# A two-layer trunk with expert mixtures: requests for expert weights, the split of the tokens and the order within a group of experts are changed

## The chip, the core and the metric

The kernel runs on one core of a Trainium2 chip. The metric is the time of one execution on the device in microseconds. TensorE (PE) multiplies matrices into PSUM banks, VectorE (DVE), ScalarE (ACT) and GpSimd (POOL) work element by element, and SyncE (SP) issues nearly all transfers, in the order of its queue; a request whose target is not yet free holds up all behind it. All arithmetic is in float32.

## The reference

There are 256 context tokens and 256 latent tokens of 1024 channels and two layers. Layer 0 mixes with attention beside a gated delta rule, layer 1 with a recurrence over the tokens; after each comes a mixture of experts, over 512 tokens in layer 0 and over the 256 latent tokens in layer 1:

```python
def hier_moe(h, w_group, b_group, w_expert, b_expert, w1, w3, w2):
    pg = softmax(h @ w_group + b_group)          # 4 groups of experts, the best is taken
    pg_top, g_idx = lax.top_k(pg, 1)
    pe = softmax(take_along_axis(h @ w_expert + b_expert, sel, axis=1))   # the group's 8 experts
    pe_top, e_loc = lax.top_k(pe, 2)             # the two best
    wts = pg_top * pe_top / jnp.sum(pe_top, -1, keepdims=True)
    ...                                          # tokens sorted by expert
        hid = jax.nn.silu(xb @ w1[e]) * (xb @ w3[e])
        return out.at[toks].add((hid @ w2[e]) * ws[:, None]), None
```

w1 and w3 of an expert are 1024 x 512, w2 is 512 x 1024: 2 MiB each, 6 MiB an expert, 32 experts a layer.

## The kernel before

A pool of 21 tiles of 1 MiB (128 partitions x 2048 float32, called s in the rows) holds the activations h, the weights and other large data. An expert matrix fills two tiles; `weight` (L163) issues one request for each. Tiles are given out by a planner, which also fixes the order of the instructions on each engine: it takes the code's order as priority and works with its own estimate of the times. `issue_after` and a dependency set by hand bind it.

Between mixer and mixture, `project_out` (L904; for layer 1 the end of `mixer1`, L1646) asks for the output weights, the rows of shift and scale (`rows`, L377), and the first expert weights (`moe_ahead`, L628: six matrices in layer 0, w1, w3 and w2 of experts 0 and 1, and five in layer 1). While the projection runs, `tokens` (L389) makes the logits and the transposed tokens, `raw`. Its inner function `split` (L430) then makes the normalized, shifted tokens for each of the token tiles: a rank-one matmul of a row of ones with the shift, and a matmul of `raw` with a diagonal of the token norms, both into one PSUM bank. ACT copies the bank, rounded, to the upper half `hi` of a tile of f, and DVE subtracts it for the lower half `lo`, so that the gather can use two fast passes.

`moe` (L645) runs the router (L454; its last instruction is `last`), builds the first group's one-hot matrix P, calls `split`, then in layer 0 `sort` (L518), which orders the experts 4 to 31 by their token count (experts 0 to 3 are fixed), and `overflow`. Then come the groups, two in flight: in layer 0 pairs of experts (64 tokens each), one group of 96 and 32, and three groups of four experts (32 tokens each); in layer 1 eight groups of four. A group gathers its tokens (L681), multiplies by w1 and w3 (L705), transposes, multiplies by w2 (L729), splits the result into y and scatters it into h (L739). Within these matmuls each expert writes its own partitions of the bank, that is, it uses its own columns of PE; the four experts (or parts of 32) follow one another inside the loop over k. For w2 the order is half of the output, k, expert; for the last group of a layer it is expert, k, half (L728).

Weights are asked for expert by expert (L704, L723). For the sorted experts SP first loads the expert's number into a register (`value_load`, L772). In layer 1 the first six groups stand ahead of a loop for experts with more tokens than their place, which here runs no time, and the last two behind it; five matrices of the seventh group are asked for ahead of the loop (L798). In layer 0 the loop stands behind all groups; the next mixer's first weights (`mixer1_weights`, L1429) are asked for ahead of it.

Of the kernel before, what the change touches and what calls it, by code (L numbers as in the profile page):

```python
# [118 lines left out]
class Trunk:  # L119
# [43 lines left out]
    def weight(self, src, natural=False, eng=None):  # L163
# [11 lines left out]
        return ks  # L175

# [212 lines left out]
    def tokens(self, l, h, lo, rows):  # L389
# [40 lines left out]
        def split(last):  # L430

            f = []
            dg = self.tmp(nt * 128).rearrange("p (t n) -> p t n", t=nt)
            for t in range(nt):
                self.act(dg[:, t], self.c["ident"], AF.Copy, scale=rs[:, t:t + 1])
                f.append(self.slot().rearrange("p (i n) -> p i n", i=2))
            for i in range(2):
                half = slice(512 * i, 512 * i + 512)
                for t in range(nt):
                    ps = self.bank()  # L440
                    add = rows[st(t)][0:1, 1, 4 * i:4 * i + 4].rearrange("p k n -> p (k n)")
                    self.mm(ps, self.c["ones"][0:1], add, True, False)
                    self.mm(ps, dg[:, t], raw[t][:, half], False, True)
                    hi, lo = f[t][:, 0, half], f[t][:, 1, half]
                    if i:
                        with self.tc.issue_after(last.ins):
                            self.split(hi, lo, ps)
                    else:
                        self.split(hi, lo, ps)
            return f  # L450
# [143 lines left out]
    def job(self, l, nt, sid, w, table, P):  # L594
# [30 lines left out]
        load = lambda name, g: self.weight(I[name][l, bass.ds(ereg, 1)].rearrange("o a b -> (o a) b"))  # L625
        return wt[:, :, None], load

    def moe_ahead(self, l):  # L628

        G = 2 if l == 0 else 4  # L630
        names = [(n, e + g) for e in (0, G) for n in ("moe_w1", "moe_w3", "moe_w2") for g in range(G)]
        return {(n, e): self.weight(self.I[n][l, e]) for n, e in names[:(6, 5)[l]]}

    def split(self, hi, lo, a, eng=None):

        self.act(hi.bitcast(F32R), a)
        self.tt(lo.bitcast(F32R), a, hi, OP.subtract, eng)

# [6 lines left out]
    def moe(self, l, h, lo, ahead, tokens, then=None):  # L645
# [3 lines left out]
        logits, split = tokens  # L649
        sid, w, cnt, last, chosen = self.router(logits, nt)  # L650
# [18 lines left out]
        def group(P, wt, load, caps, last=False):  # L669
# [31 lines left out]
            for i in range(2):  # L701
                ps = self.bank()
                hp.append(ps)
                W = [load(("moe_w1", "moe_w3")[i], g) for g in range(G)]  # L704
# [18 lines left out]
            W = [load("moe_w2", g) for g in range(G)]  # L723
            pw = [self.bank() for _ in range(2)]
            order = [(i, k, q) for i in range(2) for k in range(4) for q in parts]
            if last:

                order = [(i, k, q) for q in parts for k in range(4) for i in range(2)]  # L728
# [18 lines left out]
        def experts(spec, last):  # L747
# [17 lines left out]
            regs = {}  # L765

            def load(name, g):
                p = cols[g]
                if p < fixed:
                    return ahead.pop((name, p), None) or self.weight(I[name][l, p])  # L770
                if p not in regs:
                    regs[p] = nc.sync.value_load(order[0:1, p:p + 1], min_val=0, max_val=31)  # L772
                return self.weight(I[name][l, bass.ds(regs[p], 1)].rearrange("o a b -> (o a) b"))

            yield from group(P, weights[:, :, cs], load, caps, last)

        def extra():
            P = t4()
            wt, load = self.job(l, nt, sid, w, table, P)
            yield  # L780
            yield from group(P, wt, load, (128,))

        gens = [experts(s, i == len(specs) - 1) for i, s in enumerate(specs)]
        next(gens[0])
        ft = split(last)
        next(gens[0])
        rank = None
        if l == 0:
            sp, wp, order, rank = self.sort(nt, sid, cnt, chosen)
# [6 lines left out]
        else:  # L796
            e0 = specs[cut][0][0]
            for name, g in [(m, g) for m in ("moe_w1", "moe_w3") for g in range(4)][:5]:  # L798
                ahead[name, e0 + g] = self.weight(I[name][l, e0 + g])
# [1290 lines left out]
```

## Time and profile before

| | |
|---|---|
| median of 3 runs | 2273.4 us (2269.46 to 2273.95) |
| profiled execution | 2272.61 us, its span 2270.8 us |
| PE busy | 1849.2 us, 81% of the span |
| DVE, ACT, POOL busy | 849.9, 546.5, 363.3 us |
| read from and written to device memory | 537.66 and 34.90 MB, 252 GB/s over the span |
| requests for expert weights | 384 of 1 MiB |
| mean granted clock of TensorE | 0.852 of full speed |

Times in the rows count from the span's start. Busy time says how long an engine had an instruction in work; neighbouring matmuls overlap, so a busy PE need not be at its peak, and the duration of a run of matmuls is better read from its first start to its last end. A float32 matmul appears as two records. The granted clock (PEclk) is 1.00 at 2.4 GHz and 0.50 at 1.2 GHz. The share of the DMA engines can read 1.01.

### The profile page before, as it was taken

How to read it: one execution, taken by the hardware profiler on the slowest of the kernel's cores; microseconds unless marked ns; L12 is line 12 of the kernel's file. 1: busy time of each engine (PE TensorE's matmuls, PEld its weight loads, DVE VectorE, ACT ScalarE, POOL GpSimd, SP SyncE). 2: the span in 40 equal slices, each digit the busy share in tenths (PEclk: the TensorE clock that was granted, in tenths of full speed). 3: DMA queues.
4: the chain of work that ended last, by engine and by line, in shares of the span. 5: the costliest groups of instructions: out<-in, count | busy, mean ns of one | idle time of the engine just before them, and what ended most of it. 6: DMA issues, size and time to landing. Idle time of an engine off the chain costs nothing.

```text
span 2270.8 us, 32125 instructions
## 1 busy us (share of the span) xinstructions
PE 1849.2 (81%) x12738; PEld 1020.6 (45%) x12738; DVE 849.9 (37%) x1889; ACT 546.5 (24%) x1110; POOL 363.3 (16%) x603
## 2 busy tenths in 40 slices
PE   5996888898999898998599698789786877666577
PEld 2443566566444343443245466657675422222222
DVE  3357345533332223221644856565822311111101
ACT  3363223320211111111324524425221100000000
POOL 1034145310000000000403732234400000000000
PEclk7998889899899999999797686578575788788789
DMA  9631132760099999999252544372774399999995
GB/s 308 225 130 38 43 112 100 268 245 22 12 422 421 421 421 421 421 421 392 73 195 79 186 140 154 121 237 77 277 268 178 133 422 421 421 422 421 384 422 248
DMA packets 161226, 574.70 MB, mean 253 GB/s; under 512 B 26218, under 2 KB 61073, under 8 KB 108593
## 3 DMA queue, kind: packets, MB, share of 16 engines
q1 hardware_dynamic: 158704, 572.36, 65.1%
q8 instruction: 102, 1.67, 0.3%
q10 hardware_dynamic: 2369, 0.25, 0.1%
q14 instruction: 51, 0.42, 0.1%
HBM read 537.66 MB, written 34.90 MB: 252 GB/s over the span
## 4 chain that ended last, share of the span: by engine, by line
DMA 19%; PE 18%; DVE 8%; ACT 3%; issue 2%; POOL 1%; SPq 0%; ACTq 0%; DVEq 0%; POOLq 0%
PE b L202 18%; DMA s<-in_moe_w 16%; DVE s L184 3%; ACT t L197 2%; DVE kb L184 1%; DVE t L184 1%; DVE s L193 1%; PE b L213 1%; ACT s L197 1%; DMA s<-vD 1%; POOL s L184 1%; DMA s<-in_rk_wr 1%; POOL t L184 0%; DVE s L1977 0%; DMA s<-kD 0%
## 5 line engine op out<-in xcount | busy, mean ns | idle before, releaser
L202 PE MATMUL b<-s 64*64 64x64 f32 (+10 forms) x5840 | 671.0, 324 | 103.2 <-DVE s L193 27.1
L202 PEld LDWEIGHTS b<-s 128*64 128x64 f32 (+5 forms) x5840 | 444.3, 184 | 331.9 <-issue 173.9
L202 PE MATMUL b<-s,kb 128*32 128x512 f32 (+1 forms) x2112 | 365.4, 649 | 80.3 <-DMA s<-in_moe_w 80.3
L202 PE MATMUL b<-s,t 128*32 128x512 f32 (+4 forms) x1544 | 349.5, 566 | 50.4 <-DMA s<-in_moe_w 24.6
L197 ACT ACTIVATE t<-b 128x512 f32<-128x512 f32 (+3 forms) x161 | 91.3, 571 | 715.5 <-PE b L202 422.1
L202 PEld LDWEIGHTS b<-s,t 128*32 128x32 f32 (+2 forms) x1544 | 153.6, 148 | 212.0 <-issue 129.1
L202 PEld LDWEIGHTS b<-s,kb 128*32 128x32 f32 (+1 forms) x2112 | 97.3, 125 | 324.8 <-issue 207.9
L197 ACT ACTIVATE s<-b 128x256 f32<-128x256 f32 (+6 forms) x194 | 101.0, 526 | 463.4 <-PE b L202 425.7
L202 PE MATMUL b<-t,s 128*128 128x512 f32 (+3 forms) x592 | 160.4, 424 | 19.5 <-ACT s L197 8.9
L184 DVE TENSOR_TENSOR s<-b,s 128x512 fp32r<-128x512 f32 (+2 forms) x86 | 52.3, 626 | 274.5 <-ACT s L197 266.1
L193 DVE SCALAR_TENSOR_TENSOR s<-b,mcol,s 128x256 f32<-128x256 f32 x296 | 120.9, 476 | 80.8 <-PE b L202 80.6
L213 PE MATMUL b<-cst,t 128*128 128x128 f32 (+1 forms) x466 | 80.3, 304 | 75.6 <-DVE t L193 35.1
L202 PEld LDWEIGHTS b<-t,s 128*128 128x128 f32 (+2 forms) x592 | 100.7, 205 | 79.5 <-ACT s L197 26.3
L184 POOL TENSOR_TENSOR t<-t 128x256 f32<-128x256 f32 (+1 forms) x20 | 21.0, 1052 | 651.9 <-DMA hD<-s 534.0
L213 PEld LDWEIGHTS b<-cst,t 128*128 128x128 f32 (+1 forms) x466 | 57.4, 162 | 121.4 <-issue 42.9
L193 DVE SCALAR_TENSOR_TENSOR t<-t,wc,b 128x512 f32<-128x512 f32 x21 | 15.7, 747 | 201.2 <-PE b L202 201.2
L213 PE MATMUL b<-cst,s 128*128 128x128 f32 (+1 forms) x332 | 60.7, 323 | 23.6 <-DVE s L184 14.8
L193 DVE SCALAR_TENSOR_TENSOR t<-t,b 128x512 f32<-128x512 f32 x21 | 14.4, 688 | 169.6 <-ACT t L197 169.6
L197 ACT ACTIVATE kb<-b 128x512 f32<-128x512 f32 (+2 forms) x92 | 49.9, 545 | 100.2 <-PE b L202 66.8
L202 PE MATMUL b<-t,cst 128*128 128x512 f32 (+6 forms) x64 | 37.2, 699 | 44.0 <-POOL t L184 20.0
L213 PEld LDWEIGHTS b<-cst,s 128*128 128x128 f32 (+1 forms) x332 | 46.3, 168 | 39.4 <-issue 28.5
L202 PE MATMUL b<-s,cs 128*32 128x512 f32 x384 | 54.9, 655 | 6.5 <-DMA s<-in_ada_w 6.0
(240 smaller groups left out, 1637.4 us busy)
## 6 DMA issues: line engine op xcount, KB each, us to landing
s<-in_moe_w SPq DMA_DIRECT2D x384, 1024.0 KB, 19.8
s<-in_ada_w SPq DMA_DIRECT2D x48, 1024.0 KB, 8.5
s<-in_hy_w_in SPq DMA_DIRECT2D x8, 1024.0 KB, 5.0
sD<-s SPq DMA_DIRECT2D x8, 1024.0 KB
s<-zD SPq DMA_DIRECT2D x8, 1024.0 KB, 7.6
s<-sD SPq DMA_DIRECT2D x8, 1024.0 KB, 10.1
s<-in_hy_w_out SPq DMA_DIRECT2D x4, 1024.0 KB
s<-in_rk_wk SPq DMA_DIRECT2D x4, 1024.0 KB, 8.7
```

Source lines behind the costliest of these rows:

```text
L184: (eng or self.nc.vector).tensor_tensor(out=out, in0=a, in1=b, op=op)
L193: self.nc.vector.scalar_tensor_tensor(out, a, s, b, op0=op0, op1=op1)
L197: self.nc.scalar.activation(out, a, func, bias=bias, scale=scale)
L202: return self.nc.tensor.matmul(out, lhsT, rhs, start=start, stop=stop, skip_group_check=skip)
L213: self.nc.tensor.transpose(out, a, self.c["ident"][:n, :n])
```

## The change

`weights` loads several matrices side by side: the first tile of each, then the second of each. `moe_ahead` uses it; layer 0 asks for the same six matrices, layer 1 for w1 and w3 of four experts. `split` becomes a generator: the first half of the channels (matmuls and `hi`) is traced ahead of the router, its `lo` and the second half's matmuls behind it. In layer 0 all weights of experts 2 and 3 are asked for ahead of `sort`. A register load is tied behind the request that was traced before it (`late_load`). Ahead of layer 1's loop four matrices are asked for instead of five. The w2 order is k, half, expert for all groups.

```diff
+    def weights(self, srcs):
+        n = srcs[0].shape[1]
+        nk, per = srcs[0].shape[0] // 128, 2048 // n
+        out = [[] for _ in srcs]
+        for k0 in range(0, nk, per):
+            for ks, src in zip(out, srcs):
+                t = self.slot().rearrange("p (k n) -> p k n", n=n)
+                self.nc.sync.dma_start(t, src.rearrange("(p k) n -> p k n", p=128)[:, k0:k0 + per])
+                ks += [t[:, i] for i in range(per)]
+        return out
...
-        def split(last):
-            f = []
+        def split():
+            f = [self.slot().rearrange("p (i n) -> p i n", i=2) for _ in range(nt)]
             dg = self.tmp(nt * 128).rearrange("p (t n) -> p t n", t=nt)
             for t in range(nt):
                 self.act(dg[:, t], self.c["ident"], AF.Copy, scale=rs[:, t:t + 1])
-                f.append(self.slot().rearrange("p (i n) -> p i n", i=2))
             for i in range(2):
                 half = slice(512 * i, 512 * i + 512)
+                pss = [self.bank() for _ in range(nt)]
                 for t in range(nt):
-                    ps = self.bank()
                     add = rows[st(t)][0:1, 1, 4 * i:4 * i + 4].rearrange("p k n -> p (k n)")
-                    self.mm(ps, self.c["ones"][0:1], add, True, False)
-                    self.mm(ps, dg[:, t], raw[t][:, half], False, True)
-                    hi, lo = f[t][:, 0, half], f[t][:, 1, half]
+                    self.mm(pss[t], self.c["ones"][0:1], add, True, False)
+                for t in range(nt):
+                    self.mm(pss[t], dg[:, t], raw[t][:, half], False, True)
+                    self.act(f[t][:, 0, half].bitcast(F32R), pss[t])
+                last = yield
+                for t in range(nt):
                     if i:
                         with self.tc.issue_after(last.ins):
-                            self.split(hi, lo, ps)
+                            self.tt(f[t][:, 1, half].bitcast(F32R), pss[t], f[t][:, 0, half], OP.subtract)
                     else:
-                        self.split(hi, lo, ps)
-            return f
+                        self.tt(f[t][:, 1, half].bitcast(F32R), pss[t], f[t][:, 0, half], OP.subtract)
+            yield f
...
     def moe_ahead(self, l):
         G = 2 if l == 0 else 4
-        names = [(n, e + g) for e in (0, G) for n in ("moe_w1", "moe_w3", "moe_w2") for g in range(G)]
-        return {(n, e): self.weight(self.I[n][l, e]) for n, e in names[:(6, 5)[l]]}
+        names = ("moe_w1", "moe_w3", "moe_w2")[:3 - l]
+        return {(n, g): w for n in names for g, w in enumerate(self.weights([self.I[n][l, g] for g in range(G)]))}
...
+    def late_load(self, ap, top):
+        ins = self.nc.cur_bb.bb.instructions
+        n = len(ins)
+        prev = next(i for i in reversed(ins) if i.engine == mybir.EngineType.SP)
+        v = self.nc.sync.value_load(ap, min_val=0, max_val=top)
+        first = next(i for i in ins[n:] if i.engine == prev.engine)
+        self.tc.add_manual_dep(first, prev.name, ...)
+        return v
...
         logits, split = tokens
+        split = split()
+        next(split)
         sid, w, cnt, last, chosen = self.router(logits, nt)
...
-                W = [load(("moe_w1", "moe_w3")[i], g) for g in range(G)]
+                W = loads(("moe_w1", "moe_w3")[i])
...
-            W = [load("moe_w2", g) for g in range(G)]
+            W = loads("moe_w2")
             pw = [self.bank() for _ in range(2)]
-            order = [(i, k, q) for i in range(2) for k in range(4) for q in parts]
-            if last:
-                order = [(i, k, q) for q in parts for k in range(4) for i in range(2)]
+            order = [(i, k, q) for k in range(4) for i in range(2) for q in parts]
...
+        regs = {}
+        def fetch(name, cols):
+            if (name, cols[0]) in ahead:
+                return [ahead.pop((name, p)) for p in cols]
+            srcs = []
+            for p in cols:
+                if p < fixed:
+                    srcs.append(I[name][l, p])
+                    continue
+                if p not in regs:
+                    regs[p] = self.late_load(order[0:1, p:p + 1], 31)
+                srcs.append(I[name][l, bass.ds(regs[p], 1)].rearrange("o a b -> (o a) b"))
+            return self.weights(srcs)
...
         next(gens[0])
-        ft = split(last)
+        split.send(last)
+        ft = split.send(last)
         next(gens[0])
         rank = None
         if l == 0:
+            for name in ("moe_w1", "moe_w3", "moe_w2"):
+                ahead.update({(name, p): x for p, x in zip((2, 3), fetch(name, (2, 3)))})
             sp, wp, order, rank = self.sort(nt, sid, cnt, chosen)
...
-            e0 = specs[cut][0][0]
-            for name, g in [(m, g) for m in ("moe_w1", "moe_w3") for g in range(4)][:5]:
-                ahead[name, e0 + g] = self.weight(I[name][l, e0 + g])
+            cols = specs[cut][0]
+            for name in ("moe_w1",):
+                ahead.update({(name, p): w for p, w in zip(cols, fetch(name, cols))})
```

## Rows read from the trace of the kernel before

**Rows 1.** The page, 40 slices of the span: what the transfers moved.
```profile
GB/s 308 225 130 38 43 112 100 268 245 22 12 422 421 421 421 421 421 421 392 73 195 79 186 140 154 121 237 77 277 268 178 133 422 421 421 422 421 384 422 248
```
**Rows 2.** Stretches: their length, each engine's busy time (instructions), granted clock, DMA share, GB/s.
```profile
497.00:621.30 124.30, 113.00 (x394) 73.22 (x395) 41.41 (x141) 17.27 (x32) 4.83 (x4) 0.90 0.04 11
...
621.30:1061.30 440.00, 397.28 (x2155) 183.86 (x2153) 122.04 (x282) 61.50 (x105) 0.00 (x0) 1.00 1.01 419
...
1084.00:1088.00 4.00, 3.43 (x15) 2.79 (x16) 2.33 (x6) 0.51 (x1) 0.00 (x0) 1.00 0.08 31
...
2244.00:2248.00 4.00, 4.00 (x14) 1.17 (x14) 0.00 (x0) 0.00 (x0) 0.00 (x0) 1.00 0.27 113
```
**Rows 3.** SP's queue in time order, 461 to 622 us: start, length, line, transfer.
```profile
461.00 89.08 SPq L173 DMA_DIRECT2D s<-in_moe_w  x12
...
561.94 0.29 SPq L1416 DMA_DIRECT2D t<-in_rk_ln_b  x1
621.28 0.85 SPq L173 DMA_DIRECT2D s<-in_moe_w  x2
```
**Rows 4.** The register loads of L772: nanoseconds min/median/max, first and last start in us.
```profile
L772 SPq TENSOR_LOAD <-o_int x28: 262/264/477, 604.8 to 620.6; - x28
L772 SPq FUSED_REGOPS  x28: 147/147/181, 605.3 to 621.0; - x28
```
**Rows 5.** SP's waits from 480 to 700 us: us in total, times, longest.
```profile
SPq L772 <- DVE t L184: 42.9, 1, 42.9
```
**Rows 6.** PE in time order at the start of layer 0's mixture [idle before <- releaser].
```profile
558.10 1.84 PE L202 MATMUL b<-cst,t 128*128 128x1 f32 x16
...
568.87 14.02 PE L202 MATMUL b<-s,cst 1*128 1x512 f32 x16
582.82 10.72 PE L202 MATMUL b<-s,t 128*128 128x512 f32 x24
...
599.37 14.00 PE L202 MATMUL b<-s,kb 128*64 128x512 f32 x64
```
**Rows 7.** Stretches of the same place, columns as in rows 2: the granted clock.
```profile
562.00:563.00 1.00, 0.00 (x0) 0.00 (x0) 0.90 (x8) 0.22 (x1) 0.00 (x0) 0.73 0.05 12
...
568.00:582.00 14.00, 14.00 (x20) 5.81 (x20) 2.82 (x16) 0.00 (x0) 0.00 (x0) 0.50 0.00 1
...
586.00:587.00 1.00, 1.00 (x3) 0.38 (x2) 0.25 (x1) 0.42 (x1) 0.00 (x0) 0.82 0.00 0
```
**Rows 8.** PE in time order, layer 0's groups: a w2, two quads, the last w2.
```profile
694.24 7.07 PE L202 MATMUL b<-s,t 128*32 128x512 f32 x64
...
741.39 7.92 PE L202 MATMUL b<-s,kb 128*32 128x512 f32 x70
752.13 7.05 PE L202 MATMUL b<-s,kb 128*32 128x512 f32 x58 [2.82 <-DMA s<-in_moe_w]
...
891.08 7.92 PE L202 MATMUL b<-s,kb 128*32 128x512 f32 x70
...
1061.29 22.59 PE L202 MATMUL b<-s,t 128*32 128x512 f32 x64 [0.69 <-ACT t L197]
```
**Rows 9.** PE in time order, layer 1: start of the mixture and its last w2.
```profile
1773.92 1.71 PE L213 MATMUL b<-cst,s 128*128 128x128 f32 x8
...
1789.52 7.29 PE L202 MATMUL b<-s,t 128*128 128x512 f32 x12
...
2240.06 19.16 PE L202 MATMUL b<-s,t 128*32 128x512 f32 x56
```
**Rows 10.** SP's queue: the next mixer's first stores, and loads of the recurrence.
```profile
1093.45 4.24 SPq L1448 DMA_DIRECT2D hD<-s  x8
...
1723.75 1.49 SPq L1891 DMA_DIRECT2D s<-vD  x2
```
**Rows 11.** DVE behind layer 1's loop, in time order.
```profile
2149.02 0.76 DVE L184 TENSOR_TENSOR t<-cst,r_sid 128x256 fp32r<-128x256 f32 x2 [15.92 <-DMA s<-in_moe_w]
```
**Rows 12.** PE's waits from 620 to 1100 us: us in total, times, longest.
```profile
PE b L202 <- DMA s<-in_moe_w: 11.0, 6, 3.4
```

More of the change, by code (lines that the diff above doesn't have):

```diff
@@ L624, in job @@
         ereg = nc.sync.value_load(reg_t, min_val=0, max_val=31)
-        load = lambda name, g: self.weight(I[name][l, bass.ds(ereg, 1)].rearrange("o a b -> (o a) b"))
-        return wt[:, :, None], load
+        loads = lambda name: self.weights([I[name][l, bass.ds(ereg, 1)].rearrange("o a b -> (o a) b")])
+        return wt[:, :, None], loads
     def moe_ahead(self, l):
         G = 2 if l == 0 else 4
-        names = [(n, e + g) for e in (0, G) for n in ("moe_w1", "moe_w3", "moe_w2") for g in range(G)]
-        return {(n, e): self.weight(self.I[n][l, e]) for n, e in names[:(6, 5)[l]]}
+        names = ("moe_w1", "moe_w3", "moe_w2")[:3 - l]
+        return {(n, g): w for n in names for g, w in enumerate(self.weights([self.I[n][l, g] for g in range(G)]))}
     def split(self, hi, lo, a, eng=None):
@@ L637, in split @@
         self.tt(lo.bitcast(F32R), a, hi, OP.subtract, eng)
+    def late_load(self, ap, top):
[4 more added lines that the diff above has]
+        first = next(i for i in ins[n:] if i.engine == prev.engine)
+        self.tc.add_manual_dep(first, prev.name, mybir.DependencyInfo(mybir.DependencyClass.NoSync,
+                                                                      mybir.DependencyReason.DATA), reason="late_load")
+        return v
     def pick(self, out, onehot, hi, lo, start=True, stop=True):
@@ L667, in moe, with group @@
         half = lambda i: slice(512 * i, 512 * i + 512)
-        def group(P, wt, load, caps, last=False):
+        def group(P, wt, loads, caps):
             G = len(caps)
@@ L745, in group, with experts @@
                     yield
-        def experts(spec, last):
+        regs = {}
[11 more added lines that the diff above has]
+            return self.weights(srcs)
+        def experts(spec):
             cols, caps = spec
@@ L764, in experts @@
             yield
[L765 to L775, printed above, removed]
+            yield from group(P, weights[:, :, cs], lambda name: fetch(name, cols), caps)
         def extra():
             P = t4()
-            wt, load = self.job(l, nt, sid, w, table, P)
+            wt, loads = self.job(l, nt, sid, w, table, P)
             yield
-            yield from group(P, wt, load, (128,))
-        gens = [experts(s, i == len(specs) - 1) for i, s in enumerate(specs)]
+            yield from group(P, wt, loads, (128,))
+        gens = [experts(s) for s in specs]
         next(gens[0])
-        ft = split(last)
+        split.send(last)
+        ft = split.send(last)
         next(gens[0])
```

## The prediction, made before the changed kernel was run

> **What bounds the kernel now.** I began with the page's forty slices [rows 1]. The DMA engines run at about 421 GB/s in slices 11 to 17 and 32 to 37 and far lower elsewhere. These two stretches are the two expert mixtures. Each must read 32 experts of 6 MiB, 192 tiles of 1 MiB; at 421 GB/s a tile takes 2.49 us, so a mixture costs 478 us of transfer however it is ordered. What can be won is time in which the queue stands still while weights are wanted, and work that is left once the last tile is there.
>
> The second view was SP's queue at the first mixture's start [rows 3]. Twelve tiles (experts 0 and 1) are asked for between 461 and 550 us; the next request goes out at 621.28 us. In the stretch from 497 to 621.3 us DMA is 4% busy, in the 440 us behind it 101% [rows 2]. Two things fill the end of that hole: SP waits 42.9 us for the sorted order [rows 5], then issues 28 register loads [rows 4] back to back from 604.8 to 621.3 us, though the next 12 tiles (experts 2 and 3) need no register. TensorE (PE), meanwhile, finishes the logits at 559.94 us, waits for the router, and only then does the split's matmuls [rows 6].
>
> The third view was PE at the mixtures' ends. In all other groups of four column parts, 64 down-projection records take 7.07 us, 0.110 us each, because neighbours in the order use different column parts. The last group runs part by part: 22.59 us for the same 64 in layer 0 [rows 8], and 19.16 us for the last 56 in layer 1 [rows 9]. There DMA ends at about 2245.1 us (113 GB/s over the 4 us from 2244 [rows 2] is 1.1 us at full rate), and PE at 2259.2 us.
>
> **Which time the sum uses.** The profiled execution took 2272.6 us with a span of 2270.8 us; the median of the runs is 2273.4 us, 0.8 us more. I work on 2272.6.
>
> **Split ahead of the router, layer 0.** Eight rank-one matmuls of the row of ones (16 records) and eight of the raw tokens (16 records) move. Before, the ones begin at 568.87 us and cost 14.02 us, 0.876 us a record; the raw tokens' records end 2.1 us (eight gather records) before 593.54 us, at 591.4 us; expert matmuls start at 599.37 us [rows 6], 8.0 us later. In the new order the ones can start at 559.94 us. The granted clock stays 1.00 for 2.7 us of PE's pause, then falls to 0.50 (1.2 GHz) [rows 7]. It stays there through 14 us in which PE is busy with the ones alone, and comes back to 1.00 (2.4 GHz) about 3.4 us after the raw tokens start at 582.82 us. I take it that the ones don't hold the clock: 2.8 us at 0.43 us a record does 6.4 records, the other 9.6 take 8.4 us (571.1 us); the router's two matmuls 1.2 us (572.3); raw tokens 3.4 us at 0.50 for 3.9 records, then 12.1 at 0.43, 5.2 us: 580.9 us. Experts start at 588.9 us, **10.5 us earlier**. If the clock held throughout, it would be 32 x 0.43 + 1.2 from 559.94, 574.9 us, 16.5 us earlier; if the planner gives the moved matmuls no earlier place, 0. The split's activations now stand ahead of the router's exponentials on ACT, and the first half's four subtractions among its DVE work: at 0.6 to 0.7 us each, at most 2.8 us on a router that is no longer last.
>
> By the Trainium skill, page "TensorE: Matmul & The Clock Gate", section "What's actually happening", activity releases the throttle, with busy-ness of PE as the measure; by that rule the ones, which keep PE busy, would hold 2.4 GHz. The trace speaks against it: 14.0 of 14.0 us busy at 0.50 [rows 7]. It is the first rival below.
>
> **Requests ahead of the ranking, and register loads one by one.** The pool has 21 tiles. During the split it holds h (2), f (4) and experts 0 and 1 (12), so only 3 are free once rows and raw are done with, at 571 to 581 us. Eight more come as the first group's w1 and w3 are used, from 592 to 603 us, and the last after its w2. So the early request fills the hole in part only, and I count tiles at a later point: the first quad's start. Before, this is 741.39 us, and its matmuls stall until 752.13 us [rows 8] for the 15th tile of that quad in load order. The three groups ahead of the quad take 36 tiles, so this is tile 51 behind the restart, and landings follow 625.1 + 2.49 n us: at 741.39 us 46.7 tiles had landed, 10.7 of them the quad's. After, PE arrives 10.5 us earlier and saves perhaps another 1.4 us of short stalls, at 729.5 us, and every tile that can be full is: 21 less h, f and one y is 14. That makes 36 + 14 = 50 landed at 729.5 us, where the old line has (729.5 - 625.1) / 2.49 = 41.9: 8.1 tiles, 20.2 us. A full pool then stops DMA until the quad's first tiles are used (w1's first half, 3.5 us), about 3 us. So the **DMA lead is 17 us**. From there DMA decides again: three pairs and a quad need 60 x 2.49 = 149.5 us of transfer, and PE went from quad to quad (741.39 to 891.08 us) in 149.7 [rows 8]. Where the pool gives no more than PE's shift, the lead is 10.5 us; without slot limits it would be at most 50 us (621.3 less 571).
>
> The 28 register loads cost SP 0.57 us each; they now stand among 168 requests, where SP mostly waits for credit or a free tile: nothing. Were this cover gone, 16 us would come back.
>
> **Side by side, and the order by k.** The same tiles land, but the first half of each expert first: PE needs tile 12 of a quad, not 15, to begin w3, and frees tiles half a set at a time. While DMA is the bound this pays nothing in the middle. At the end it does. After the last tile only 13 of 32 matmuls remain, 26 records x 0.110 = 2.9 us. Layer 1: 2259.2 - 2245.1 = 14.1 us becomes 2.9, **11.2 us**. Layer 0: last expert tile at 625.1 + 180 x 2.49 = 1073.3 us, PE's end 1061.29 + 22.59 = 1083.9 us [rows 8]; 10.6 us becomes 2.9, **7.7 us**. No row has k outside and the two banks alternating; its record may cost anything between 0.110 us and the lone 0.353 us. I take 0.110, since neighbours still differ in column part.
>
> Layer 0 in sum: 17 + 7.7, about 25 us. Behind it come the scatter, up to the next mixer's first store at 1093.45 us [rows 10], 9.6 us that don't change, and the weights of that mixer, whose transfers end at about 1084.3 us (31 GB/s over the 4 us from 1084 [rows 2] is 0.3 us at full rate) and after at 1067, when the scatter ends at 1068: hidden, by 1 us.
>
> **Layer 1's start.** PE ends its transposes at 1775.6 us, and the raw tokens end 1.1 us before 1796.81, at 1795.7 [rows 9]. After: 8 records of ones at 0.876 (7.0 us), the router's pair 1.1, raw tokens 6.2 as before: 1789.9 us, **5.8 us** (10.5 with the clock held). From the first w1 half on DMA is continuous, so the last tile lands 5.8 us earlier.
>
> **Second mixture's weights ahead.** 16 tiles are asked for instead of 10. SP asks for a tile when the pool has one, as before, so I count no gain. Six more may stand in front of the recurrence's loads at 1723.75 us [rows 10], up to half of them at that moment: bounds 0 and +7.5 us (3 x 2.49). I take 0, since the pool also gave tiles to the rest of this group before. Ahead of the loop 8 tiles instead of 10 are loaded. The loop waits for their landing (DVE 15.92 us for DMA [rows 11]), so it opens two tiles earlier with DMA as long idle: 0, at worst +5.
>
> **Sum:** 25 + 5.8 + 11.2 = 42 us; 2272.6 - 42 = 2230.6, on the median 2231.
>
> **Rivals.** (A) The ones hold the clock: layer 0's lead grows by 6.0, layer 1's by 4.7, so 2220. For it: no row has the ones at full clock to begin with. Against: 14 us of busy PE without a rise. (B) The early request meets a full pool, and DMA gains PE's shift only: 10.5 + 7.7 + 17 = 35, 2238; with the state loads late by up to 7.5, 2245. For it: 21 tiles, 18 taken. Against: at 741 us only 10.7 of 14 were used. (C) Slower: the k order with alternating banks loses the overlap of column parts. Layer 0 has four groups of 64 records (+0.243 us each, 15.5 us a group) and nine pairs of 32 at 0.22 (+0.13, 4.2 us a group): 100 us on PE. PE went from 599.37 to 1061.29 us with 11.0 us of waits for weights [rows 12]; without these and with a last w2 of 7 us it would end at 588.9 + 451 + 7 = 1047 us, so with the loss at 1147, 63 us later than 1083.9. With layer 1's start 5.8 earlier and its tail as before: 2330. It is slower than before once 43 of these 100 us are lost (1047 + 43 is 5.8 us behind 1083.9), from about 0.21 us a record of four parts. For it: the last groups show how dear lost overlap is. Against: w1 and w3 rotate the same way at 0.11. (D) It doesn't do what it says: the planner puts the requests and matmuls where they were, and only the tails shorten: 7.7 + 11.2, 2254.
>
> **How the numbers follow.** Main case 0.57, its own range 2222 to 2240; A 0.13; B 0.15; C 0.05; D 0.06; 0.04 for a re-planned second mixer that eats the gain (half no change, half slower). The range 2210 to 2250 leaves out C, most of D and those. A difference under 0.2% (4.5 us) can't be told from none here. Faster 0.91 (main, A, B, D), same 0.02, slower 0.07.
>
> **What would show it.** Right: 12 expert requests before the first register load; a register load just ahead of its own request; the first expert matmul near 589 us; 14 tiles of the first quad landed at its start; the last w2 in 7 to 9 us in both layers; PE done some 3 us after the last tile. Wrong: DMA standing still between 600 and 720 us, a w2 record at 0.2 us or more in a group of four parts, the first expert matmul later than 595 us, or a second mixer that grew by more than 5 us.

## The result, and the profile after

The changed kernel took 2237.3 us (median of 4 runs, 2231.0 to 2248.1) where the kernel before took 2273.5: a ratio of 0.985, 95% interval 0.9825 to 0.9876. The prediction was 2231 us, range 2210 to 2250: right in sign and range, 6 us too fast. Run twice more beside the experiments, the changed kernel was 31.5 and 29.9 us faster than the kernel before on the same chip (2270.2 to 2238.7, 2269.7 to 2239.8; ratios 0.9865, interval 0.9839 to 0.9891, and 0.9864, interval 0.9836 to 0.9891). So some 33 us were won, not 42. Rival B's 2238 us lies nearer than the main case, but by luck: it counted 10.5 us for the split, which gave 6.3, and nothing for the requests, which gave 7.5 together with the register loads. The profiled execution took 2232.8 us with a span of 2231.0.

PE at the start of layer 0's mixture, in time order (start, length in us; the idle time before and what ended it in brackets), as in [rows 6]:

```profile
556.20 1.84 PE L214 MATMUL b<-cst,t 128*128 128x1 f32 x16
561.71 0.35 PE L225 MATMUL b<-cst,t 72*128 72x72 f32 x1 [3.67 <-DMA t<-in_rk_ln_b]
562.00 7.19 PE L214 MATMUL b<-s,cst 1*128 1x512 f32 x8
569.12 6.22 PE L214 MATMUL b<-s,t 128*128 128x512 f32 x8
575.18 0.61 PE L214 MATMUL b<-t,cst 128*128 128x128 f32 x4
575.71 2.84 PE L214 MATMUL b<-s,cst 1*128 1x512 f32 x6
...
591.13 14.01 PE L214 MATMUL b<-s,kb 128*64 128x512 f32 x64
```
The logits end at 558.04 us (556.20 + 1.84). The first half's rank-one records come ahead of the router's pair (575.18), as the diff wants, but begin 4 us late: in PE's queue a transpose of the next mixer's small vectors stands first, and it waits 3.67 us for their transfer. Before, the same wait lay inside the wait for the router.

SP's queue and register loads (nanoseconds min/median/max, first and last start), as in [rows 3, 4]:

```profile
580.50 79.17 SPq L185 DMA_DIRECT2D s<-in_moe_w  x26
```
```profile
L659 SPq TENSOR_LOAD <-o_int x28: 262/268/487, 618.4 to 984.2; - x28
```
Requests restart at 580.5 instead of 621.28 us, and the register loads are spread over 366 us. Yet the stretches (columns as in [rows 2]) show DMA pausing again and again until 736 us, most of all from 656 to 660; from the restart to the first quad it runs at 0.88 (first row):

```profile
580.00:729.91 149.91, 138.61 (x748) 67.52 (x746) 52.05 (x143) 26.00 (x45) 0.00 (x0) 1.00 0.88 351
594.00:621.30 27.30, 25.03 (x126) 12.35 (x124) 8.76 (x43) 4.67 (x8) 0.00 (x0) 1.00 0.85 334
640.00:660.00 20.00, 17.94 (x92) 10.40 (x96) 9.00 (x24) 4.64 (x8) 0.00 (x0) 1.00 0.83 344
656.00:660.00 4.00, 4.00 (x29) 2.88 (x31) 2.38 (x8) 1.09 (x2) 0.00 (x0) 1.00 0.11 41
740.00:1060.00 320.00, 288.38 (x1500) 129.69 (x1493) 81.85 (x188) 42.80 (x73) 0.00 (x0) 1.00 1.01 419
2212.00:2216.00 4.00, 2.88 (x10) 0.53 (x12) 0.00 (x0) 0.00 (x0) 0.00 (x0) 1.00 0.46 193
2213.50:2215.00 1.50, 1.50 (x4) 0.22 (x2) 0.00 (x0) 0.00 (x0) 0.00 (x0) 1.00 0.29 120
2215.00:2215.70 0.70, 0.23 (x1) 0.00 (x0) 0.00 (x0) 0.00 (x0) 0.00 (x0) 1.00 0.00 0
```
PE at the first quad and at the end of the last group, layer 0; the router's pair, a w2 and the last w2 in layer 1, as in [rows 8, 9]; SP's first store of the next mixer, as in [rows 10]:

```profile
729.91 13.94 PE L214 MATMUL b<-s,kb 128*32 128x512 f32 x128
...
1045.51 3.40 PE L214 MATMUL b<-s,t 128*32 128x512 f32 x12 [0.69 <-ACT t L209]
1049.50 4.38 PE L214 MATMUL b<-s,t 128*32 128x512 f32 x24 [0.59 <-DMA s<-in_moe_w]
1054.46 1.90 PE L214 MATMUL b<-s,t 128*32 128x512 f32 x4 [0.58 <-DMA s<-in_moe_w]
1056.95 1.90 PE L214 MATMUL b<-s,t 128*32 128x512 f32 x4 [0.58 <-DMA s<-in_moe_w]
1059.51 3.62 PE L214 MATMUL b<-s,t 128*32 128x512 f32 x20 [0.65 <-DMA s<-in_moe_w]
...
1756.27 1.12 PE L214 MATMUL b<-t,cst 128*128 128x64 f32 x4 [3.60 <-DVE t L196]
...
1791.01 7.07 PE L214 MATMUL b<-s,t 128*32 128x512 f32 x64
...
2215.76 3.62 PE L214 MATMUL b<-s,t 128*32 128x512 f32 x20 [0.53 <-DMA s<-in_moe_w]
```
```profile
1072.70 4.22 SPq L1481 DMA_DIRECT2D hD<-s  x8
```
The first quad no longer stalls: its 128 records take 13.94 us without a break. The last w2 now follows its tiles: a short wait at each, and 20 records behind the last one.

Absolute times differ between executions before the change even begins (the logits end between 555.7 and 561.4 us in all kernels but one), and so does the second mixer. So the kernels are compared by five distances: from the end of the logits to the first expert matmul (A) and to the first store of the next mixer (B); from that store to PE's last transposes of layer 1's tokens (C); from there to the first expert matmul of layer 1 (D); and from that to the end of PE's last w2 (E). Each is the difference of two rows like those above, in the profiled execution, in us:

| kernel | median us | A | B | C | D | E |
|---|---|---|---|---|---|---|
| before | 2273.5 | 39.4 | 533.5 | 682.2 | 25.4 | 458.2 |
| changed, three comparisons | 2237.3, 2238.7, 2239.8 | 33.1, 33.1, 33.2 | 514.7, 514.8, 514.9 | 676.9, 679.6, 688.2 | 20.8, 21.1, 19.0 | 449.1, 448.8, 449.4 |
| e1 new order alone | 2255.7 | 39.4 | 529.3 | 675.8 | 25.5 | 451.9 |
| e2 old order back | 2257.9 | 33.2 | 524.4 | 680.5 | 21.0 | 459.1 |
| e3 split behind the router | 2246.1 | 39.4 | 521.1 | 678.7 | 24.8 | 448.7 |
| e5 loads not tied | 2240.3 | 33.1 | 514.9 | 679.5 | 21.0 | 449.0 |
| e6 128 rows deep | 2233.0 | 28.6 | 510.6 | 679.2 | 20.7 | 449.4 |
| e7 expert by expert | 2245.8 | 33.2 | 515.9 | 685.6 | 21.0 | 451.4 |
| e8 vectors later | 2240.6 | 32.2 | 514.0 | 681.0 | 21.1 | 449.0 |
| e9 8 tiles ahead | 2235.6 | 33.1 | 514.7 | 676.5 | 21.0 | 449.2 |
| e10 vectors earlier, 128 rows | 2241.9 | 27.5 | 509.2 | 689.8 | 20.7 | 449.3 |
| e11 neither request nor tie | 2244.9 | 33.1 | 522.2 | 682.2 | 20.8 | 449.2 |

A, B and E repeat within 0.6 us in the three executions of the changed kernel, so effects of 1 us can be read in them; D repeats within some 2 us. C can't be read so: it differs by 11 us between these three.

### The profile page after: what moved, and what is told of

Read it like the earlier page. It is cut to its first block, busy times and chain, and to the rows that moved or that the text cites. A ratio compares the mean times of both kernels' runs of the same rounds, so it can differ in the third digit from the quotient of the medians.

```text
span 2231.0 us, 32127 instructions
## 1 busy us (share of the span) xinstructions
PE 1835.9 (82%) x12738; PEld 1004.4 (45%) x12738; DVE 849.8 (38%) x1889; ACT 546.6 (25%) x1110; POOL 363.6 (16%) x603
## 4 chain that ended last, share of the span: by engine, by line
DMA 21%; PE 16%; DVE 8%; ACT 3%; issue 2%; POOL 1%; SPq 0%; ACTq 0%; DVEq 0%; POOLq 0%
DMA s<-in_moe_w 19%; PE b L214 15%; DVE s L196 3%; ACT t L209 2%; DVE kb L196 2%; DVE t L196 1%; DVE s L205 1%; ACT s L209 1%; PE b L225 1%; POOL s L196 1%; DMA s<-in_rk_wr 0%; DMA s<-zD 0%; DMA s<-kD 0%; DVE s L2010 0%; POOL t L196 0%
## 5 line engine op out<-in xcount | busy, mean ns | idle before, releaser
L214 PE MATMUL b<-s 64*64 64x64 f32 (+10 forms) x5840 | 659.4, 317 | 107.7 <-DVE s L205 27.0
L214 PEld LDWEIGHTS b<-s 128*64 128x64 f32 (+5 forms) x5840 | 434.5, 178 | 335.2 <-issue 172.2
L214 PE MATMUL b<-s,kb 128*32 128x512 f32 (+1 forms) x2112 | 379.7, 643 | 66.9 <-DMA s<-in_moe_w 66.9
L214 PE MATMUL b<-s,t 128*32 128x512 f32 (+4 forms) x1544 | 341.4, 540 | 37.7 <-DMA s<-in_moe_w 16.2
L214 PEld LDWEIGHTS b<-s,t 128*32 128x32 f32 (+2 forms) x1544 | 147.6, 143 | 195.3 <-issue 109.3
L214 PEld LDWEIGHTS b<-t,s 128*128 128x128 f32 (+2 forms) x592 | 99.3, 203 | 78.5 <-ACT s L209 25.5
L196 POOL TENSOR_TENSOR t<-t 128x256 f32<-128x256 f32 (+1 forms) x20 | 21.0, 1051 | 633.5 <-DMA hD<-s 515.1
L225 PE MATMUL b<-cst,s 128*128 128x128 f32 (+1 forms) x332 | 60.7, 324 | 24.2 <-DVE s L196 14.8
## 6 DMA issues: line engine op xcount, KB each, us to landing
s<-in_moe_w SPq DMA_DIRECT2D x384, 1024.0 KB, 19.8
```

What stands on the lines that cost most here:

```text
L196: (eng or self.nc.vector).tensor_tensor(out=out, in0=a, in1=b, op=op)
L214: return self.nc.tensor.matmul(out, lhsT, rhs, start=start, stop=stop, skip_group_check=skip)
L225: self.nc.tensor.transpose(out, a, self.c["ident"][:n, :n])
```

## The experiments

Batches of four shared a chip and the runs of the kernel before: e1, e2, e3 and e5; e6, e7, e8 and the changed kernel; e9, e10, e11 and the changed kernel.

**e1: the kernel before with the new order of w2 alone.**
```diff
-            order = [(i, k, q) for i in range(2) for k in range(4) for q in parts]
-            if last:
-                order = [(i, k, q) for q in parts for k in range(4) for i in range(2)]
+            order = [(i, k, q) for k in range(4) for i in range(2) for q in parts]
```


> The kernel before with one edit: the down-projection of every group goes by k, half, expert, the last group included; loads stay expert by expert, the split stays behind the router, register loads stay in front. Theory 1 (the order alone shortens both ends): layer 0 ends 7.7 us earlier (first store of the next mixer at 1085.8 instead of 1093.45 us), layer 1 another 11.2 us: 2254.6 us. Theory 2 (the order pays only with tiles that come side by side, since k = 0 needs the seventh of eight tiles): at most half of it, 2264 us. Theory 3 (alternating banks lose the overlap of column parts): a w2 record of four parts at 0.2 us or more, and no gain.

2255.7 us, ratio 0.9949 (0.9931 to 0.9967). B falls by 4.2, E by 6.3: 10.5 us, between theories 1 and 2. Theory 3 is dead (52 records in 7.05 us). PE at layer 0's end:
```profile
1059.05 3.37 PE L202 MATMUL b<-s,t 128*32 128x512 f32 x8 [0.69 <-ACT t L197]
1065.49 3.51 PE L202 MATMUL b<-s,t 128*32 128x512 f32 x4 [3.07 <-DMA s<-in_moe_w]
1070.45 7.05 PE L202 MATMUL b<-s,t 128*32 128x512 f32 x52 [1.46 <-DMA s<-in_moe_w]
```
With tiles expert by expert, 52 of 64 records wait for the last expert's first tile, and an estimated 4.6 us are left behind its second (7.05 less the 2.49 us of a tile).

**e2: the changed kernel with the old order of w2**, that is, e1's edit taken back.

> The changed kernel with the old order of the down-projection (half, k, expert; in the last group of a layer expert, k, half). Theory 1 (the order is worth the 18.9 us that the prediction gave it): 2256 us. Theory 2 (as the changed kernel's trace has it): its last w2 of layer 0 begins at 1045.5 us and ends at 1063.1, with 22.6 us of matmuls it would end at 1068.1, 5.0 us later; that of layer 1 begins at 2204.6 and ends at 2219.4, and would end at 2227.2, 7.8 us later: 2250 us.

2257.9 us, ratio 0.9954 (0.9938 to 0.9971). B grows by 9.7, E by 10.1 us: 19.8, near theory 1's number, for a reason it did not have. Beside the slow order part by part, the first expert now waits for its second tile, which lands fifth of eight:
```profile
1046.75 3.62 PE L214 MATMUL b<-s,t 128*32 128x512 f32 x8 [0.69 <-ACT t L209]
1053.21 20.83 PE L214 MATMUL b<-s,t 128*32 128x512 f32 x56 [2.84 <-DMA s<-in_moe_w]
```

**e7: the changed kernel with its tiles loaded expert by expert.**
```diff
-        for k0 in range(0, nk, per):
-            for ks, src in zip(out, srcs):
+        for ks, src in zip(out, srcs):
+            for k0 in range(0, nk, per):
```


> The changed kernel with each expert's two tiles loaded one behind the other, expert by expert, as before; the order k, half, expert stays. Theory 1 (the order of the loads carries what the order of the matmuls alone did not give: e1 gained 4.3 and 6.3 us at the two ends, taking the new order out of the changed kernel cost 9.7 and 10.1): the ends lose 5.4 and 3.8 us, 2246 us, and 52 records remain for the last tiles instead of 20. Theory 2 (it changes only which records wait: from the seventh tile 7.05 us of records, against 2.49 us and 3.62 us behind the eighth, 0.9 us at each end): 2239 us.

B grows by 1.2 and E by 2.3 us: theory 2's size at the first end, more at the second. The median (2245.8, ratio 0.9887, interval 0.9858 to 0.9916) is 7.1 us above the changed kernel's beside it and hits theory 1's 2246, but by luck: B and E have only half of it, and what the rest is stays open (the two profiled executions differ by 13.4 us, 3.8 of it ahead of the logits' end and 6.0 in C). The ends add up from both sides: new order alone 4.2 + side by side 1.2 = 5.4 us in layer 0, 6.3 + 2.3 = 8.6 of the measured 9.1 in layer 1.

**e3: the changed kernel with the split behind the router.**
```diff
         split = split()
-        next(split)
         sid, w, cnt, last, chosen = self.router(logits, nt)
...
         next(gens[0])
+        next(split)
         split.send(last)
```


> The changed kernel with all matmuls of the split traced behind the router, as before. Theory 1 (PE's start carries through to the end of layer 0, since the pool of tiles ties transfers to the matmuls that free them): experts start about 8 us later in layer 0 (599 us), the end of layer 0 moves by as much, layer 1 loses another 4.7 us: 2250 us. Theory 2 (in layer 0 the earlier requests alone set the lead, and PE catches up): only layer 1's 4.7 us are lost, 2242 us. Theory 3 (the split's place does nothing): 2237 us.

2246.1 us, ratio 0.9905 (0.9884 to 0.9926). A grows by 6.3, B by 6.4, D by 4.0 us. Theory 1: what PE loses at the start of layer 0 is still lost at its end, nearly 500 us later. The first quad and the end show the same shift on the way (734.33 us is 178.1 behind the logits, against 171.9):
```profile
734.33 13.94 PE L214 MATMUL b<-s,kb 128*32 128x512 f32 x128
...
1064.10 3.62 PE L214 MATMUL b<-s,t 128*32 128x512 f32 x20 [0.64 <-DMA s<-in_moe_w]
```

**e5: plain register loads in the changed kernel. e11: these, and no request ahead of the ranking.**
```diff
-                    regs[p] = self.late_load(order[0:1, p:p + 1], 31)
+                    regs[p] = nc.sync.value_load(order[0:1, p:p + 1], min_val=0, max_val=31)
```
and in e11 besides
```diff
-            for name in ("moe_w1", "moe_w3", "moe_w2"):
-                ahead.update({(name, p): x for p, x in zip((2, 3), fetch(name, (2, 3)))})
```


> The changed kernel with plain register loads, not tied behind the request traced before them; the planner now sets 12 of the 28 among the requests for experts 2 and 3 and 16 behind these. Theory 1 (the tie gives what 28 loads of 0.57 us cost): layer 0 ends 16 us later, 2253 us. Theory 2 (only loads that hold up a request whose tile is free cost anything, and the pool is full for most of that time): layer 0 ends 0 to 5 us later, 2237 to 2242 us.

> The changed kernel without the request for experts 2 and 3 ahead of the ranking and with plain register loads; the planner then sets all 28 of them ahead of the thirteenth expert request, as before the change. (Without the tie alone, e5, layer 0 ended 0.3 us later.) Theory 1 (either of the two is enough, and together they give what the split and the tails leave unexplained of layer 0, 18.9 - 6.3 - 5.3 to 6.7): layer 0 ends 6 to 7 us later, first store 521 us behind the logits, and the first quad waits for a tile again: 2244 us. Theory 2 (the pool ties transfers to PE in any case): under 2 us. Theory 3 (all 16 us of the loads come back): 531 us, 2254 us.

e5: 2240.3 us, ratio 0.9889 (0.9852 to 0.9925), B later by 0.2 us: theory 2. Its 28 loads stand between 594.5 and 613.7 us, in the stretch in which the changed kernel's SP waits for PE to free tiles, and DMA moves as much there (348 GB/s against 334):
```profile
L783 SPq TENSOR_LOAD <-o_int x28: 262/266/493, 594.5 to 613.2; - x28
```
```profile
594.00:621.30 27.30, 25.03 (x126) 12.22 (x123) 8.04 (x38) 5.27 (x9) 0.00 (x0) 1.00 0.89 348
```
e11: 2244.9 us, ratio 0.9898 (0.9871 to 0.9924), B later by 7.5 us, with the first quad waiting again: theory 1. Here requests restart at 612.85 us, 32 us later than in the changed kernel, and then DMA doesn't pause:
```profile
594.00:621.30 27.30, 25.04 (x125) 12.43 (x122) 8.75 (x43) 4.67 (x8) 0.00 (x0) 1.00 0.28 106
640.00:660.00 20.00, 17.04 (x84) 10.01 (x83) 6.28 (x15) 4.68 (x8) 0.00 (x0) 1.00 1.01 422
```
```profile
732.27 12.27 PE L214 MATMUL b<-s,kb 128*32 128x512 f32 x102
745.97 3.62 PE L214 MATMUL b<-s,kb 128*32 128x512 f32 x26 [1.43 <-DMA s<-in_moe_w]
```
A start 32 us earlier is worth 7.5 us; for much of the rest the changed kernel's pool is full (between 594 and 621 us its SP waits five times for PE to free a tile, up to 12.0 us). e11 takes out the request and the tie together, and its 28 loads stand ahead of the restart (596.4 to 612.2 us), so 7.5 us is the worth of both; no run has the tie without the request. With the request, the loads cost nothing even untied (e5).

**e6: the rank-one matmuls made 128 rows deep. e8 and e10: the wait for the small vectors moved.**
```diff
+            o128 = self.small([128, 128], f"o128_{l}")
+            self.act(o128, self.c["ones"], AF.Copy, scale=1.0 / 128)
...
-                    add = rows[st(t)][0:1, 1, 4 * i:4 * i + 4].rearrange("p k n -> p (k n)")
-                    self.mm(pss[t], self.c["ones"][0:1], add, True, False)
+                    add = rows[st(t)][:, 1, 4 * i:4 * i + 4].rearrange("p k n -> p (k n)")
+                    self.mm(pss[t], o128, add, True, False)
```


> The changed kernel with the rank-one matmuls of the split replaced by matmuls over all 128 rows (a matrix of 1/128 times the row, which every partition holds): same columns, same number of records, 128 rows in place of 1. Theory 1 (matmuls of one row don't bring TensorE's clock up, those of 128 rows do): of the first 8 records (7.19 us at 0.50) some 4 run at full clock, 5.2 us, and the raw tokens behind them take 3.4 instead of 6.2 us; experts start about 4.8 us earlier in layer 0 (28.3 us behind the logits instead of 33.1) and 1 to 2 us earlier in layer 1: 2231 us. Theory 2 (the clock doesn't see how many rows a matmul uses): experts at 33.1 us behind the logits, 2237 us.

A falls by 4.5 us (28.6 where 28.3 was expected), B by 4.1: theory 1, except that layer 1 gains nothing. PE in e6, and its granted clock in the same stretch (seventh column), first of the changed kernel, then of e6:
```profile
565.27 6.32 PE L214 MATMUL b<-s,o 128*128 128x512 f32 x8
571.42 3.60 PE L214 MATMUL b<-s,t 128*128 128x512 f32 x8
```
```profile
562.00:569.00 7.00, 7.00 (x9) 2.48 (x8) 4.31 (x24) 0.20 (x1) 0.00 (x0) 0.50 0.01 2
...
572.00:575.00 3.00, 3.00 (x6) 1.23 (x5) 1.24 (x2) 1.08 (x2) 0.00 (x0) 0.63 0.00 0
```
```profile
565.30:568.30 3.00, 3.00 (x5) 1.44 (x5) 2.85 (x16) 0.20 (x1) 0.00 (x0) 0.50 0.02 5
568.30:571.30 3.00, 3.00 (x5) 1.12 (x4) 1.53 (x9) 0.00 (x0) 0.00 (x0) 0.61 0.00 0
571.30:574.80 3.50, 3.50 (x9) 1.52 (x8) 1.38 (x2) 1.79 (x3) 0.00 (x0) 1.00 0.00 0
```
Both start at 1.2 GHz. With one row, PE is 7.0 of 7.0 us busy at 0.50 and the clock rises only inside the raw tokens' records; with 128 rows it has risen before they start. The columns, the records and the busy share are the same; the two kernels differ in the rows of these matmuls (in both operands), in one more instruction on ACT, and in when the clock rose. The Trainium skill, page "TensorE: Matmul & The Clock Gate", section "What's actually happening", speaks of how busy PE is; by that the two would be alike, and here they are not.

As a whole e6 took 2233.0 us (ratio 0.9839, 0.981 to 0.9868) beside 2238.7 for the changed kernel (0.9865). The intervals overlap, so that it is faster rests on A and B, not on the whole time.

e8 traces the vectors' requests behind the split's first half, in layer 0; e10 asks for them ahead of the output projection and has e6's edit too:
```diff
-        self.mixer1_ahead()
         self.moe(0, h, 0, ahead, tokens, self.mixer1_weights)
...
         next(split)
+        if l == 0:
+            self.mixer1_ahead()
```


> The changed kernel with the next mixer's small vectors (their requests and the one transpose that makes columns of them) traced behind the first half of the split instead of ahead of it, in layer 0 alone. In the changed kernel TensorE waits 3.67 us for these requests before it begins the split. Theory 1 (that wait is what the prediction's 10.5 us for the split missed): experts start 3.7 us earlier or more, at 29 us or less behind the logits instead of 33.1, and layer 0 ends as much earlier: 2233 us. Theory 2 (the router, 17.1 us behind the logits in the changed kernel, is next, or the pool of tiles holds the transfers): experts less than 1.5 us earlier, 2237 us.

> The changed kernel with rank-one matmuls made 128 rows deep (as in e6) and the next mixer's small vectors asked for ahead of the output projection, so that their transpose lies long before the logits. Theory 1 (the two waits add up: 4.5 us of clock and 3.7 us of waiting for the vectors): experts 24 to 25 us behind the logits, layer 0 ends 8 us earlier than in the changed kernel, 2229 us. Theory 2 (as in e8, the router's two matmuls, which stand between the halves of the split and can't run before about 11.5 us, are next): experts 27 to 29 us behind the logits, 2233 us.

e8: 2240.6 us, ratio 0.9876 (0.9848 to 0.9905). A falls by 0.9 us only: theory 2's number. The 3.67 us wait is gone, and PE waits for the router instead, whose pair of matmuls (first row) stands ahead of the second half. The pair still comes 5.6 us earlier than in the changed kernel (11.5 us behind the logits instead of 17.1), but from it to the experts 20.7 us pass instead of 16.0, since the clock falls in the middle of the one-row records and is at 0.50 for 10 us in which PE is busy:
```profile
569.89 0.68 PE L214 MATMUL b<-t,cst 128*128 128x128 f32 x4 [2.60 <-DVE r_e L196]
570.50 5.80 PE L214 MATMUL b<-s,cst 1*128 1x512 f32 x8
```
```profile
570.00:571.00 1.00, 1.00 (x5) 0.67 (x6) 0.96 (x5) 0.00 (x0) 0.00 (x0) 1.00 0.00 0
572.00:582.00 10.00, 10.00 (x13) 3.69 (x12) 3.13 (x7) 2.04 (x4) 0.00 (x0) 0.50 0.43 123
```
e10 has the same wait at 4.14 us, and A at 27.5, 1.1 us below e6: theory 2 again. It is no faster (2241.9, ratio 0.9878, interval 0.9853 to 0.9903): its logits end at 566.9 us, 5.5 us or more behind all other kernels'. The wait has only been moved, for the vectors' transpose now stands ahead of the output projection in PE's queue:
```profile
494.52 0.35 PE L225 MATMUL b<-cst,t 72*128 72x72 f32 x1 [7.29 <-DMA t<-in_rk_a]
```
The two also show whether one-row records keep the clock up. In both, the first half follows the logits without a pause, with the clock at 1.00 until then; in e8 it is at 0.50 from 559 us on (first row), and in e10, with 128 rows in the same place, it stays at 1.00 (second row):
```profile
559.00:562.00 3.00, 3.00 (x5) 0.68 (x3) 2.16 (x14) 1.49 (x5) 0.67 (x1) 0.50 0.25 43
```
```profile
567.00:570.00 3.00, 3.00 (x7) 1.11 (x7) 1.75 (x14) 1.61 (x6) 1.04 (x1) 1.00 0.28 43
```

**e9: 8 tiles instead of 16 asked for ahead of the second mixture.**
```diff
-        names = ("moe_w1", "moe_w3", "moe_w2")[:3 - l]
+        names = ("moe_w1", "moe_w3", "moe_w2")[:3 - 2 * l]
```


> The changed kernel with 8 tiles (w1 of four experts) instead of 16 asked for ahead of the second mixture's start. Theory 1 (the prediction's: SP asks whenever the pool has a tile, so the list asked for ahead makes no difference): the stretch from the experts' start in layer 1 to PE's last w2 record stays at 449 us, the second mixer at 679 us (its length varied from 676 to 682 us between kernels with the same queue there): 2238 us. Theory 2 (the extra 8 tiles stood in front of the recurrence's loads, up to 7.5 us): the mixer shrinks to 672 us. Theory 3 (they gave the mixture its lead): the stretch grows by up to 8 x 2.49 us, 20 us.

2235.6 us, ratio 0.9857 (0.9832 to 0.9882). D and E are unchanged, C lies at the edge of its scatter: theory 3 is dead. Between theories 1 and 2 it can't be told: theory 2's 7.5 us in C are less than the 11 us by which C scatters, and the ratios overlap (0.9864 for the changed kernel beside it).

**The changed kernel again**, twice:

> The changed kernel once more, unchanged, so that the three kernels beside it are compared on the same chip. Theory 1 (its executions differ by the clock that the second mixer is granted, and by nothing else): the profile's marks in layer 0 stand within 0.5 us of the first profile's, counted from the end of the logits (experts +33.1, first store of the next mixer +514.7 us), and times scatter between 2231 and 2248 us. Theory 2 (the first profile was an exception): marks that differ by more than 2 us.

> The changed kernel once more, so that the three beside it are compared on one chip: experts 33.1 us behind the logits, first store of the next mixer 514.7 us behind them, 2238 us.

A and B came out within 0.3 us: the first profile was no exception. The two profiled executions differ by 7.8 us of span (2231.5 and 2239.3), and C by 8.7. That the second mixer's clock alone makes the difference, as theory 1 has it, fits (a mean of 0.76, 0.74 and 0.73 over C in the three executions, for 676.9, 679.6 and 688.2 us) but is not shown.

## Why the prediction was right, step by step, and why its gain was 9 us too large

In the profiled execution 39.8 us of span went: 18.9 in B (25 predicted), 4.6 in D (5.8), 9.1 in E (11.2), which is 32.6, and 1.9 ahead of the logits' end and 5.3 in C, neither of them forecast. Three comparisons of medians gave 36.2, 31.5 and 29.9, 32.5 in the mean: what B, D and E explain (A lies within B).

- **Split ahead of the router, 10.5 us: 6.3** (A; e3 the same from the other side). The step that failed is "the ones can start at 559.94 us", with the logits: they started 4.0 us behind them, behind a transpose of other work in PE's queue. The rest, 33.1 - 4.0 = 29.1 us, is the 29.0 that the sum had, in part by luck. The sum had all sixteen ones ahead of the raw tokens and 6.4 of them at 2.4 GHz at the start, before the clock fell. In the run the clock had fallen by then, the first half's eight ran at 1.2 GHz (0.90 us each), and the second half's at 2.4 GHz (0.47), behind the raw tokens' records, in the middle of which the clock had risen. Clearing the wait would not have given the 4 us back: in e8 the router and the clock take most of it.
- **The ones don't hold the clock:** right. e8 shows that they don't keep it up where 128 rows do (e10), and e6 that they don't bring it up where 128 rows do. Rival A's 6.0 us for the opposite were 4.5 when e6 brought it about, from a start at 1.2 GHz. One reading of the sum is off: a stretch of 1 us at 0.73 is 0.46 us at 1.00 and the rest at 0.50, so the clock fell at 562.46 us, not at 562.7, which makes the sum's ones 0.2 us longer.
- **DMA lead of 17 us: about 13.9**, 6.4 from the split (e3) and 7.5 from the requests with the loads (e11), if the two add up; the last tile of layer 0 comes 13.6 us earlier (501.5 us behind the logits instead of 515.1, see below). The account by tiles held: 50 tiles had landed when the quad began (351 GB/s over 149.9 us is 52.6 MB), it did not stall, and DMA lost 3 us at its start (257 GB/s from 728 to 736 us). But the quad began 171.9 us behind the logits, not 169.6 as in the sum, since PE had started 4.1 us later than forecast and made up a part of it only. Of rival B, the full pool is there (DMA pauses until 736 us), but a gain of PE's shift alone would have been 6.4.
- **Register loads hidden, "were this cover gone, 16 us would come back":** the first half was right, the second not borne out. Untied they cost 0.2 us (e5); with the early request gone too, 7.5 come back (e11), not 16.
- **Ends: 18.9 us predicted, about 14 measured.** Layer 0: 18.9 - 13.9 = 5.0 (7.7); layer 1 9.1 (11.2). The 2.9 us behind the last tile (26 records at 0.110) is the term that was mis-sized. Read as the sum read it, layer 1's transfers end at 2213.8 us (0.46 of the 4 us from 2212) and PE at 2219.4: 5.6 us. The work itself, 20 records, takes 3.6 us, 0.18 each. The other 1.9 us come from taking the bytes for transfers that stop at full rate: they end slowly, at 0.29 from 2213.5 to 2215.0 us, and PE is released at 2215.8, 0.8 us behind the last data; in both repeats it is the same within 0.2 us. Why the last transfers run at a fraction of the rate is open. In layer 0 the before side was wrong too: e1's eighth tile can be placed at 1072.9 us (1070.45 + 2.49), 515.1 behind the logits, where the sum had 513.4, so that 8.8 us behind the last tile became 3.6, not 10.6 became 2.9.
- **Layer 1's start, 5.8 us: 4.6.** The sum has no wait for the router between the halves: PE waits 3.60 us for it, and its pair comes 6.7 us behind the transposes (1756.27), 0.9 later than before. D's scatter is larger than the 1.2 us that are missing, so this is their likely cause and not a measured one.
- **The signs.** "Last w2 in 7 to 9 us" did not come: it takes 17.6 us in layer 0 (1045.51 to 1063.13) and 14.8 in layer 1. The sum's own numbers do not give it in layer 0: a w2 that begins at 1061.29 and ends 2.9 us behind a tile at 1073.3 takes 14.9. Of the signs of being wrong, "DMA standing still between 600 and 720 us" did come in part (0.11 from 656 to 660 us): SP then waits for PE to free tiles. A second mixer longer by more than 5 us came in one of three executions (688.2 to 682.2), which C's scatter makes worthless as a sign.
- **Side by side pays nothing in the middle; second mixture ahead 0:** the first is right (e7's B); of the second, e9 shows that 16 tiles gave no lead, and can't tell what they cost the mixer. Rival C's loss did not appear (64 records in 7.07 us, 1791.01). Rival D is excluded by A.

## What to carry to other kernels

Where a pool of tiles bounds the transfers, an earlier request is worth what the pool has free, and what moves the matmuls that free the tiles counts in full: here 32 us of earlier requests, with the register loads out of their way, gave 7.5, and 6.3 us of earlier matmuls gave 6.4. When work is moved to "as soon as its input is there", read in the engine's queue what stands ahead of it and waits for something else, and what will be next once that is cleared: e8 cleared a wait of 3.67 us and won 0.9. And a rate averaged over a stretch does not say when the last transfer ends; look at shorter stretches. An order of loads and an order of use belong together: the new order alone gave 10.5 us, the old order among the new loads cost 19.8.

## What the runs showed of the hardware

Matmuls of one row left TensorE at 1.2 GHz through 7.0 us of unbroken work (0.50 from 562 to 569 us); matmuls of 128 rows with as many columns brought 2.4 GHz in the course of the same eight records (0.50, 0.61 and 1.00 in e6's three stretches). One-row records that followed the logits without a pause lost 2.4 GHz (0.50, e8), and records of 128 rows in their place kept it (1.00, e10). At 2.4 GHz six rank-one records took 2.84 us, 0.47 each (the row at 575.71; the clock in the first row below), against 0.90 at 1.2 GHz.

At the end of layer 1's stream of 1 MiB tiles the DMA share was 0.29 for 1.5 us, and the waiting matmuls were released 0.8 us behind the last data (2213.50 to 2215.76).

Long waits went with a lower clock: in the stretch from 1800 to 2180 us DMA runs at 1.00 in both kernels (416 GB/s), but with tiles expert by expert PE waits for them 34 times, 2.7 us in the mean, and its mean clock is 0.83 (e7, third row), and side by side it waits 64 times, 1.1 us in the mean, and the clock is 0.90 (the changed kernel, second row). In all it also waits less (71.5 us instead of 91.0; last two rows), so that the length of the single wait makes the difference is not shown. DMA sets the time there in both.

```profile
576.00:580.00 4.00, 4.00 (x10) 1.42 (x9) 2.95 (x15) 0.95 (x2) 0.00 (x0) 1.00 0.00 0
...
1800.00:2180.00 380.00, 275.15 (x1458) 87.02 (x1461) 41.57 (x101) 29.51 (x53) 0.00 (x0) 0.90 1.00 416
```
```profile
1800.00:2180.00 380.00, 253.76 (x1486) 84.73 (x1484) 43.59 (x107) 32.65 (x59) 0.00 (x0) 0.83 1.00 416
```
```profile
PE b L214 <- DMA s<-in_moe_w: 71.5, 64, 1.5
```
```profile
PE b L214 <- DMA s<-in_moe_w: 91.0, 34, 4.1
```
